# Seven block products in place of eight for 20 chunks of a decoder trunk's last down projection

## The chip, the cores and the metric

The kernel runs on one core of a Trainium2 chip. The metric is the device time of one execution in microseconds (us), and lower is better. A core has a matrix engine (TensorE, PE in the profile, with its weight loads shown as PEld), a vector engine (VectorE, DVE), a scalar engine (ScalarE, ACT), a general-purpose engine (GpSimd, POOL) and a queue engine (SyncE, SP) that issues most of the DMAs here. Each engine works through its own instructions in the order in which the program wrote them, and waits on the others through semaphores.

## The reference, cut to what matters

A two-layer decoder trunk on 256 tokens with width 2048: layer 0 is a gated MLP mixer and a convolutional FFN, then shared keys and values, layer 1 is an attention and a second convolutional FFN, then a final RMSNorm. All of it is float32. The change lies in the last matrix product of all, `w_down` of layer 1:

```python
def conv_ffn(xn, w_up, conv_w, conv_b, w_down):
    h = xn @ w_up                                   # (256, 2048) @ (2048, 11264)
    hp = jnp.pad(h, ((0, 0), (CONV_W - 1, 0), (0, 0)))
    h = sum(hp[:, k:k + S] * conv_w[k] for k in range(CONV_W)) + conv_b
    gate, val = jnp.split(h, 2, axis=-1)
    return (jax.nn.silu(gate) * val) @ w_down       # (256, 5632) @ (5632, 2048)
...
    h = h + conv_ffn(rmsnorm(h, f_norm[l]), f_w_up[l], f_conv_w[l], f_conv_b[l], f_w_down[l])
...
    return rmsnorm(h, final_norm)
```

## The kernel before, in words

**Precision.** Every float32 operand is split into two parts of a shorter format (float32r): a rounded part "hi" and a remainder "lo". A product is the sum of three matmuls: hi x hi, hi x lo and lo x hi. The activations of the second FFN lie in the tile `H` as 44 K-tiles of 128 rows, each with 256 tokens of hi and 256 of lo (`ffn_h`, L642).

**The stream of weights.** All weights come through one `Stream` (L44 to L115) of chunks, 128 x 1024 floats or 512 KB each. SP loads a chunk six items ahead (L77) into one of four `raw` buffers. Three items ahead the chunk is split (L80 to L97): ACT copies it to `whi` (L95), then DVE writes the remainder to `wlo` (L96). Each of `whi` and `wlo` has four buffers, so the split for item i+3 can begin only when PE has finished with the buffer of item i-1. Then PE multiplies item i (L110), and after it `advance` (L63) lets each pending generator emit one more step, up to its next `yield`: the work behind a product (evictions, norms, residuals) is written out in this order among the splits, on the same DVE and ACT queues.

**The down projection of layer 1** (L982 to L985) has 2048 output columns. Three blocks of 512 columns go through `tok_block` (L228 to L272), 22 chunks each, 66 in all. A chunk holds 256 rows of K (two K-tiles) times 512 columns, and its products with the tokens are eight blocks: two K-tiles, two halves of the tokens and two halves of the columns. Each is a 128 x 128 stationary operand of H times a moving 128 x 256 piece of the chunk, in three matmuls: 24 a chunk (a few at the start are 512 wide instead, `wide_next`, L188). The sums stand in a PSUM tile `ps` of two banks, one of three such buffers (`main_ps`, L170). The last 512 columns go in two halves through `short_block` and `last_block` (22 chunks).

**Behind a block** runs `final(blk)` (L407): for each half of the tokens DVE adds `ps` into the residual `h` (L404), ACT takes its square with a running sum (L405), and DVE multiplies by the gain (L416). `output` (L469) closes the kernel.

**GpSimd** is nearly idle: it fills a few constants, masks (L892, `affine_select`) and issues some DMAs of the attention.

**X1**, a tile of 16 x 512 float32r a partition, holds the normed input of the up projection; after the last up product nothing reads it.

Of the kernel before, what the change touches and what calls it, by code (L numbers as in the profile page):

```python
# [22 lines left out]
KF = FFN // P  # L23
NH = 16
CHUNK = 1024
# [6 lines left out]
PAD = 64  # L32
FEAT_AT, TOK_AT = 0, 32
PITCH = 320


C_ANORM, C_KVNORM, C_BNORM, C_FNORM, C_AVNORM = 0, 16, 32, 48, 80
# [6 lines left out]
class Stream:  # L44
# [4 lines left out]
        self.items, self.pending = [], []  # L49
        self.raw, self.parts = {}, {}  # L50

    def chunk(self, src, mult, at, at_load=None, at_split=None, rows=(1, 1), place=None):


        self.items.append((src, mult, at_load, at_split, at, rows, place))

    def then(self, at_load=None, at_split=None, at_mult=None):
        self.items.append((None, at_mult, at_load, at_split, 0, None, None))

    def start(self, gen):  # L60
        self.pending.append(gen)
# [4 lines left out]
                self.pending.remove(g)  # L66

    def _load(self, i):
        src, _, at_load, _, _, _, place = self.items[i]
# [7 lines left out]
        self.nc.sync.dma_start(raw, src)  # L77
        self.raw[i] = raw

    def _split(self, i):  # L80
        if self.items[i][3]:
            self.items[i][3]()
        raw = self.raw.pop(i, None)
        if raw is None:
            return
        at, (n, pitch) = self.items[i][4:6]
        hi, lo = (self.pool.tile([P, CHUNK + PAD], F32R, name=k, tag=k)[:, at:at + CHUNK] for k in ("whi", "wlo"))
# [7 lines left out]
        self.nc.scalar.activation(h, raw, AF.Copy)  # L95
        self.nc.vector.tensor_tensor(l, raw, h.bitcast(F32), op=OP.subtract)  # L96
        self.parts[i] = (hi, lo)  # L97
# [20 lines left out]
class Phase:  # L118
# [22 lines left out]

    def temp(self, key, shape, dtype=F32, bufs=2):
        return self.pool.tile(shape, dtype, name=f"{self.name}_{key}", tag=f"{self.name}_{key}", bufs=bufs)


def build(ctx, tc, d, out):
    nc = tc.nc
# [3 lines left out]
    small = ctx.enter_context(tc.tile_pool(name="small", bufs=1))  # L151
# [6 lines left out]
    X1 = const.tile([P, KD, 2 * T], F32R, name="X1")  # L158
# [17 lines left out]
    def column(i):  # L176
        return col[:, i:i + 1]


    def mm(o, a, b, start, stop):  # L180
        nc.tensor.matmul(o, a, b, start=start, stop=stop, skip_group_check=True)  # L181
# [6 lines left out]
    def wide_next():  # L188
        return state["wide"].pop(0) if state["wide"] else 0
# [38 lines left out]
    def tok_block(src, x, done, K=KD):  # L228
        tok_blocks([(src, done)], x, K)
# [150 lines left out]
    def by_token():  # L380

        return h.rearrange("p a b -> p (a b)").rearrange("p (t f) -> p t f", t=2)
# [17 lines left out]
    def add_block(tb, cols, ps, into):  # L400

        hh = by_token()[:, tb, cols]
        sq = small.tile([P, 2, T], F32, name="sq", tag="sq", bufs=2).rearrange("p a b -> p (a b)")
        nc.vector.tensor_tensor(hh, hh, ps, op=OP.add)  # L404
        nc.scalar.activation(sq[:, :ps.shape[1]], hh, AF.Square, accum_out=into)  # L405

    def final(blk):  # L407
        def done(ps):
            ss = ph.keep("ss", [P, 2, 5])
            n = ps.shape[2]  # L410
            cols = slice(blk * 512, blk * 512 + n)
            for tb in range(2):
                add_block(tb, cols, ps[:, tb, :], ss[:, tb, blk:blk + 1])
                yield
                hh = by_token()[:, tb, cols]
                nc.vector.tensor_tensor(hh, hh, ph.keep("gains", [P, D])[:, cols], op=OP.mult)  # L416
                yield
            if blk == 3:
                v, nv = ph.keep("v", [P, 2]), ph.keep("nv", [P, 2])
                nc.vector.tensor_reduce(v, ss[:, :, :4], axis=AX.X, op=OP.add)  # L420
                nc.vector.tensor_scalar(v, v, 1.0 / D, EPS, op0=OP.mult, op1=OP.add)
                nc.vector.tensor_scalar(nv, v, -0.5, None, op0=OP.mult)
                nc.scalar.activation(warm, ones, AF.Sqrt)
        return done

    def short_block(src, x, K, done):

        n, box = K // 4, {}
        for c in range(n):
            def mult(hi, lo, c=c):  # L430
                if c == 0:
                    box["ps"] = main_ps()[:, :, :T]
                for tb in range(2):
                    short_products(box["ps"][:, tb, :], c, tb, x, K, hi, lo)
                if c == n - 1:
                    s.start(done(box["ps"]))
            s.chunk(src[c], mult, TOK_AT)
        return box
# [203 lines left out]
    def ffn_h():  # L642
        ph.open(f"ffn{state['layer']}")
        return ph.keep("H", [P, KF, 2 * T], F32R)

    def up_done(l, i):
        def done(ps, both):
            state["layer"] = l
            H = ffn_h()
            while state["scaled"] <= l:  # L650
                yield
            a = ph.temp("a", [P, 2, T])
            scaled(ps, both, a)
# [71 lines left out]
    def with_forget(src, x, done):  # L725

        box, n = {}, 0
        for nj in (3, 3, 3, 3, 2, 2):
            def mult(hi, lo, k0=n, nj=nj):
                if k0 == 0:  # L730
                    box["ps"] = main_ps()
                for j in range(nj):
                    kt = k0 + j
                    for tb in range(2):
                        for lower, part in ((0, hi), (0, lo), (1, hi)):
                            at = lower * T + tb * P
# [198 lines left out]
        return done  # L935


    state = {"normed": False, "layer": 0, "v": 0, "done": 0, "gates": 0, "mixed": 0, "scaled": 0, "wide": [8, 2]}
    cd = dram.tile([NH, T], F32, name="cd")

    nc.scalar.dma_start(col[:, :C_KVNORM], d["col"][:, :C_KVNORM])
# [27 lines left out]
    box = short_block(d["kvf_ks"], lambda: att("X2"), KD, lambda ps: iter(()))  # L969
# [85 lines left out]
```

## Time and profile before

| | |
|---|---|
| time, median of 3 runs | 2181.26 us (2180.32 to 2182.49) |
| span of the profiled execution | 2179.9 us, 1.36 us under that median |
| granted TensorE clock | 0.999 |
| matmuls | 18740 |
| HBM read | 430.72 MB, 204 GB/s over the span |

The span is from the first to the last instruction of the one profiled execution; no other time is given for that execution. In the profile's groups, L96 stands for a line of the kernel, `wlo<-raw,whi` for the tiles written and read, and the shapes are partitions x elements; "mean ns" is of one instruction. Matmuls overlap one another, so their cost is read from how many of them a stretch of time holds, and not from the duration of one.

### The profile page before, as it was taken

How to read it: one execution, taken by the hardware profiler on the slowest of the kernel's cores; microseconds unless marked ns; L12 is line 12 of the kernel's file. 1: busy time of each engine (PE TensorE's matmuls, PEld its weight loads, DVE VectorE, ACT ScalarE, POOL GpSimd, SP SyncE). 2: the span in 40 equal slices, each digit the busy share in tenths (PEclk: the TensorE clock that was granted, in tenths of full speed). 3: DMA queues.
4: the chain of work that ended last, by engine and by line, in shares of the span. 5: the costliest groups of instructions: out<-in, count | busy, mean ns of one | idle time of the engine just before them, and what ended most of it. 6: DMA issues, size and time to landing. Idle time of an engine off the chain costs nothing.

```text
span 2179.9 us, 45085 instructions
## 1 busy us (share of the span) xinstructions
PE 2170.3 (100%) x18740; PEld 2154.6 (99%) x18740; DVE 1474.8 (68%) x2085; ACT 1145.4 (53%) x1536; POOL 26.9 (1%) x46
## 2 busy tenths in 40 slices
PE   9999999999999999999999999999999999999998
PEld 9999999999999999999999999999999999999998
DVE  6696687777777755556787676678777777764444
ACT  6665555555555544444545665446555555544443
POOL 0000000000000000000001100000000000000000
PEclk9999999999999999999999999999999999999999
DMA  8686566665666666666777776567766666666664
GB/s 311 191 241 202 193 198 195 189 199 190 198 193 194 195 190 199 193 195 184 244 244 257 232 224 200 185 216 228 240 195 194 193 195 189 201 191 194 193 192 153
DMA packets 153229, 447.31 MB, mean 205 GB/s; under 512 B 25584, under 2 KB 44800, under 8 KB 152640
## 3 DMA queue, kind: packets, MB, share of 16 engines
q1 hardware_dynamic: 151488, 440.48, 64.6%
q0 software_dynamic: 1072, 3.41, 0.6%
q8 instruction: 146, 2.39, 0.5%
q10 hardware_dynamic: 464, 0.55, 0.1%
q14 instruction: 59, 0.48, 0.1%
HBM read 430.72 MB, written 13.65 MB: 204 GB/s over the span
## 4 chain that ended last, share of the span: by engine, by line
PE 99%; DMA 0%; DVE 0%; ACT 0%; SPq 0%; issue 0%; DVEq 0%
PE ps L181 98%; PE mp L913 0%; PE ps L907 0%; PE ps L908 0%; PE ps L906 0%; PE mp L912 0%; DMA mlp_vt<-a_in_v 0%; DVE h L491 0%; PE mp L376 0%; ACT whi L95 0%; ACT sq L405 0%; PE mp L181 0%; DVE h L404 0%; SPq L496 0%; DVE h L486 0%
## 5 line engine op out<-in xcount | busy, mean ns | idle before, releaser
L96 DVE TENSOR_TENSOR wlo<-raw,whi 128x1024 fp32r<-128x1024 f32 (+1 forms) x778 | 945.1, 1219 | 462.4 <-ACT whi L95 458.2
L95 ACT ACTIVATE whi<-raw 128x1024 fp32r<-128x1024 f32 (+1 forms) x778 | 819.3, 1058 | 737.8 <-PE ps L181 660.3
L181 PE MATMUL ps<-X,whi 128*128 128x256 f32 (+1 forms) x6476 | 824.0, 279 | 0.0
L181 PEld LDWEIGHTS ps<-X,whi 128*128 128x128 f32 x6476 | 776.2, 188 | 6.5
L181 PE MATMUL ps<-X,wlo 128*128 128x256 f32 x3328 | 445.3, 276 | 0.0
L181 PEld LDWEIGHTS ps<-X,wlo 128*128 128x128 f32 x3328 | 409.9, 188 | 1.6
L181 PE MATMUL ps<-whi,ffn_H 128*128 128x256 f32 (+1 forms) x1402 | 222.7, 277 | 0.0
L181 PEld LDWEIGHTS ps<-whi,ffn_H 128*128 128x128 f32 x1402 | 192.0, 188 | 0.4
L181 PE MATMUL ps<-ffn_H,whi 128*128 128x256 f32 x1408 | 173.9, 276 | 0.0
L663 DVE SCALAR_TENSOR_TENSOR ffn_c<-ffn_a,col,ffn_c 128x255 f32<-128x255 f32 x352 | 161.9, 481 | 6.4
L181 PEld LDWEIGHTS ps<-ffn_H,whi 128*128 128x128 f32 x1408 | 166.1, 188 | 0.0
L181 PE MATMUL ps<-whi,att_X 128*128 128x256 f32 (+2 forms) x970 | 164.3, 285 | 0.0
L181 PE MATMUL ps<-whi,X 128*128 128x256 f32 (+1 forms) x1000 | 157.4, 280 | 0.4 <-ACT whi L95 0.4
L181 PE MATMUL ps<-wlo,ffn_H 128*128 128x256 f32 (+1 forms) x700 | 151.3, 277 | 0.0
L181 PEld LDWEIGHTS ps<-whi,att_X 128*128 128x128 f32 x970 | 135.4, 188 | 3.5
L181 PEld LDWEIGHTS ps<-whi,X 128*128 128x128 f32 x1000 | 133.5, 188 | 1.9 <-ACT whi L95 0.6
L357 DVE TENSOR_TENSOR ffn_a<-ps,rB 128x512 f32<-128x512 f32 x76 | 52.6, 692 | 116.1 <-PE ps L181 116.1
L659 ACT ACTIVATE ffn_c<-ffn_a,col 128x256 f32<-128x256 f32 x176 | 96.3, 594 | 50.0 <-DVE ffn_a L357 50.0
L181 PEld LDWEIGHTS ps<-wlo,ffn_H 128*128 128x128 f32 x700 | 112.0, 188 | 0.1
L181 PE MATMUL ps<-wlo,att_X 128*128 128x256 f32 (+2 forms) x476 | 105.4, 286 | 0.0
L181 PE MATMUL ps<-wlo,X 128*128 128x256 f32 (+1 forms) x498 | 98.1, 280 | 0.0
L181 PE MATMUL ps<-ffn_H,wlo 128*128 128x256 f32 x704 | 94.1, 276 | 0.0
(177 smaller groups left out, 1379.2 us busy)
## 6 DMA issues: line engine op xcount, KB each, us to landing
raw<-up SPq DMA_DIRECT2D x352, 512.0 KB, 4.1
raw<-down SPq DMA_DIRECT2D x154, 512.0 KB, 4.3
raw<-a_in_u SPq DMA_DIRECT2D x32, 512.0 KB, 4.6
raw<-a_out SPq DMA_DIRECT2D x32, 512.0 KB, 3.9
raw<-b_q SPq DMA_DIRECT2D x32, 512.0 KB, 4.7
raw<-kvf_v SPq DMA_DIRECT2D x32, 512.0 KB, 4.9
raw<-b_g SPq DMA_DIRECT2D x32, 512.0 KB, 4.4
raw<-b_out SPq DMA_DIRECT2D x32, 512.0 KB, 4.2
```

The costliest lines, as they stand in the source:

```text
L95: self.nc.scalar.activation(h, raw, AF.Copy)
L96: self.nc.vector.tensor_tensor(l, raw, h.bitcast(F32), op=OP.subtract)
L181: nc.tensor.matmul(o, a, b, start=start, stop=stop, skip_group_check=True)
L357: nc.vector.tensor_tensor(a, src, rB[:, None, :].to_broadcast([P, 2, T]), op=OP.mult)
L659: nc.scalar.activation(c[:, m, :], a[:, m, :], AF.Identity, scale=w[2], bias=column(C_CONVB + l * 2 * KF + f))
L663: nc.vector.scalar_tensor_tensor(c[:, m, n:], a[:, m, :T - n], w[k], c[:, m, n:], op0=OP.mult, op1=OP.add)
```

## The change

In blocks 0, 1 and 2 of the down projection, 4 + 8 + 8 = 20 of the 66 chunks form their eight block products by a scheme of the Strassen and Winograd kind with seven. Writing A for the tokens' 2 x 2 blocks and B for the chunk's, four sums of A blocks and four of B blocks are made, and seven products of 128 x 128 by 128 x 256.

- *Sums of activations* (`sums_of_blocks`): eight pairs of K-tiles (`SUMMED`), whose four sums in hi and lo fill X1. DVE makes the sums, ACT the hi part, DVE the lo part. They are emitted in 24 steps, one behind each of the first 24 items of block 0.
- *Sums of weights* (`weight_sums`): for each of the 20 chunks GpSimd makes three subtractions from `raw` (512, 256 and 256 elements a partition) into a tile `room`.
- Such a chunk becomes two items: A splits 768 of the raw elements and makes three products (9 matmuls), B splits the 1024 elements of sums and makes four (12 matmuls). B loads nothing.
- Four of the seven products go to a second PSUM tile `m` a block; `sums_into_residual` combines its quarters with ACT and DVE and adds them to the residual in seven steps; `final(blk)` waits in program order until these steps are emitted.
- The order of the chunks is set by `order_of`. With P for a plain chunk and S for one with seven products it gives PPPPPPPPSPPSPPPSPPSPPP in block 0 and PPSPSPPSPSPPSPSPPSPSPP in blocks 1 and 2.
- In `up_done` the temporaries `a` and `c` become halves of one tile `room` of the same size.

```diff
+SUMMED = (4, 5, 8, 9, 12, 13, 16, 17)
+SUMS_ON = lambda nc: nc.gpsimd
...
+    def room(self, at):
+        return [self.pool.tile([P, CHUNK + PAD], F32R, name=k, tag=k)[:, at:at + CHUNK] for k in ("whi", "wlo")]
+
+    def two_parts(self, src, at):
+        n = src.shape[1]
+        hi, lo = self.room(at)
+        self.nc.scalar.activation(hi[:, :n], src, AF.Copy)
+        self.nc.vector.tensor_tensor(lo[:, :n], src, hi[:, :n].bitcast(F32), op=OP.subtract)
+        return hi, lo
...
+def order_of(blk):
+    some = SUMMED[:4] if blk == 0 else SUMMED
+    plain, seven = [c for c in range(KF // 2) if c not in some], list(some)
+    head = 8 if blk == 0 else 2
+    out = [(c, False) for c in plain[:head]]
+    plain = plain[head:]
+    n, m = len(plain), len(seven)
+    for i, c in enumerate(plain):
+        while len(seven) * n > (n - i - 1) * m and seven:
+            out.append((seven.pop(0), True))
+        out.append((c, False))
+    return out
...
     def final(blk):
         def done(ps):
+            while state["summed"] < min(blk + 1, 3):
+                yield
...
+    def sums_of_blocks(q, pair):
+        H = ffn_h()
+        x, f = (small.tile([P, 2, T], F32, name="sq", tag="sq", bufs=2) for _ in range(2))
+        pieces = f.rearrange("p a (b t) -> p (a b) t", b=2)
+        hi, lo = (block_sums()[:, q, :, i, :] for i in range(2))
+        hh = H[:, 2 * pair:2 * pair + 2, :].bitcast(F32)
+        nc.vector.tensor_tensor(x, hh[:, :, :T], hh[:, :, T:], op=OP.add)
...
+        nc.vector.tensor_tensor(s1, a21, a22, op=OP.add)
+        nc.vector.tensor_tensor(s3, a21, a11, op=OP.subtract)
+        yield
+        nc.vector.tensor_tensor(s2, s1, a11, op=OP.subtract)
+        nc.vector.tensor_tensor(s4, a12, s2, op=OP.subtract)
+        nc.scalar.activation(hi, pieces, AF.Copy)
+        yield
+        nc.vector.tensor_tensor(lo, pieces, hi.bitcast(F32), op=OP.subtract)
+        yield
...
+    def weight_sums(raw):
+        t = room()
+        eng = SUMS_ON(nc)
+        eng.tensor_tensor(t[:, :512].rearrange("p (a b) -> p a b", a=2), raw[:, None, :T].to_broadcast([P, 2, T]),
+                          raw[:, T:3 * T].rearrange("p (a b) -> p a b", a=2), op=OP.subtract)
+        eng.tensor_tensor(t[:, 512:768], raw[:, 512:768], t[:, :T], op=OP.subtract)
+        eng.tensor_tensor(t[:, 768:], raw[:, 768:], t[:, 512:768], op=OP.subtract)
+        return t
+
+    def seven_block(blk, src, order, done, sums_done):
...
+        def seven(c, i, first):
...
+            def split(raw):
+                held["t"] = weight_sums(raw)
+                return s.two_parts(raw[:, T:], TOK_AT)
...
+            s.chunk(src[c], mult_plain, TOK_AT, split=split)
+            s.chunk(None, mult_sums, TOK_AT, split=lambda _: s.two_parts(held["t"], TOK_AT))
...
+    def sums_into_residual(blk):
+        def done(m):
...
+            nc.scalar.activation(p1, m[:, 0, :T], AF.Copy)
+            yield
+            nc.vector.tensor_tensor(u, p1, m[:, 0, T:], op=OP.add)
+            nc.vector.tensor_tensor(x, u[:, None, :].to_broadcast([P, 2, T]),
+                                    m[:, 1, :].rearrange("p (a b) -> p a b", a=2), op=OP.add)
+            yield
+            nc.vector.tensor_tensor(u, x[:, 1, :], m[:, 1, :T], op=OP.add)
+            for tb, cols, y in ((0, right, p1), (0, left, x[:, 0, :]), (1, right, x[:, 1, :]), (1, left, u)):
+                nc.vector.tensor_tensor(hh[:, tb, cols], hh[:, tb, cols], y, op=OP.add)
+                yield
+            state["summed"] += 1
         return done
...
+    def room():
+        return ph.temp("room", [P, CHUNK])
...
-            a = ph.temp("a", [P, 2, T])
+            ac = room().rearrange("p (a m t) -> p a m t", a=2, m=2)
+            a, c = ac[:, 0], ac[:, 1]
             scaled(ps, both, a)
             yield
-            c = ph.temp("c", [P, 2, T])
...
     s.then(at_mult=between)
+    s.then(at_mult=lambda: s.start(all_sums()))
     for blk in range(3):
-        tok_block(d["down1"][22 * blk:22 * blk + 22], ffn_h, final(blk), KF)
+        seven_block(blk, d["down1"][22 * blk:22 * blk + 22], order_of(blk), final(blk), sums_into_residual(blk))
```

More of the change, by code (lines that the diff above doesn't have):

```diff
@@ L50, in __init__, with chunk @@
         self.raw, self.parts = {}, {}
-    def chunk(self, src, mult, at, at_load=None, at_split=None, rows=(1, 1), place=None):
-        self.items.append((src, mult, at_load, at_split, at, rows, place))
+    def chunk(self, src, mult, at, at_load=None, at_split=None, rows=(1, 1), place=None, split=None):
+        self.items.append((src, mult, at_load, at_split, at, rows, place, split))
     def then(self, at_load=None, at_split=None, at_mult=None):
-        self.items.append((None, at_mult, at_load, at_split, 0, None, None))
+        self.items.append((None, at_mult, at_load, at_split, 0, None, None, None))
     def start(self, gen):
@@ L68, in _load @@
     def _load(self, i):
-        src, _, at_load, _, _, _, place = self.items[i]
+        src, _, at_load, _, _, _, place, _ = self.items[i]
         if at_load:
@@ L82, in _split @@
             self.items[i][3]()
-        raw = self.raw.pop(i, None)
+        raw, split = self.raw.pop(i, None), self.items[i][7]
+        if split:
+            self.parts[i] = split(raw)
+            return
         if raw is None:
@@ L86, in _split @@
         at, (n, pitch) = self.items[i][4:6]
-        hi, lo = (self.pool.tile([P, CHUNK + PAD], F32R, name=k, tag=k)[:, at:at + CHUNK] for k in ("whi", "wlo"))
+        hi, lo = self.room(at)
         raw = raw.rearrange("p (n w) -> p n w", n=n)
@@ L423, in done, with block_sums @@
                 nc.scalar.activation(warm, ones, AF.Sqrt)
+        return done
+    def block_sums():
+        return X1.rearrange("p (q r) w -> p q (r w)", r=2).rearrange("p q (f l t) -> p q f l t", f=4, l=2)
+    def sums_of_blocks(q, pair):
[5 more added lines that the diff above has]
+        nc.vector.tensor_tensor(x, hh[:, :, :T], hh[:, :, T:], op=OP.add)
+        a11, a21, a12, a22 = (x[:, j, tb * P:(tb + 1) * P] for j in range(2) for tb in range(2))
+        s1, s2, s3, s4 = (pieces[:, i, :] for i in range(4))
+        nc.vector.tensor_tensor(s1, a21, a22, op=OP.add)
[7 more added lines that the diff above has]
+        yield
@@ new lines, in all_sums @@
+    def all_sums():
+        for q, pair in enumerate(SUMMED):
+            yield from sums_of_blocks(q, pair)
+    def weight_sums(raw):
[6 more added lines that the diff above has]
+        return t
@@ new lines, in seven_block, with three, at, plain @@
+    def seven_block(blk, src, order, done, sums_done):
+        x = ffn_h
+        box, last = {}, len(order) - 1
+        lasts = max(i for i, (_, s7) in enumerate(order) if s7)
+        def three(o, parts, stat, j, start, stop):
+            hi, lo = parts
+            for i, (lower, part) in enumerate(((0, hi), (0, lo), (1, hi))):
+                mm(o, stat[lower], part[:, j * T:(j + 1) * T], start and i == 0, stop and i == 2)
+        def at(kt, tb):
+            return [x()[:, kt, lower * T + tb * P:lower * T + (tb + 1) * P] for lower in range(2)]
+        def plain(c, i):
+            def mult(hi, lo):
+                if i == 0:
+                    box["ps"] = main_ps()
+                ps, left = box["ps"], wide_next()
+                for j in range(2):
+                    for tb in range(2):
+                        for lower, part in ((0, hi), (0, lo), (1, hi)):
+                            n, left = 512 if left > 0 else 256, left - 1
+                            for w in range(0, 512, n):
+                                mm(ps[:, tb, w:w + n], x()[:, 2 * c + j, lower * T + tb * P:lower * T + (tb + 1) * P],
+                                   part[:, j * 512 + w:j * 512 + w + n],
+                                   i == 0 and j == 0 and w == 0 and part is hi and not lower,
+                                   i == last and j == 1 and lower == 1)
+                if i == last:
+                    s.start(done(ps))
+            s.chunk(src[c], mult, TOK_AT)
+        def seven(c, i, first):
+            q = SUMMED.index(c)
+            sums = block_sums()[:, q]
+            held = {}
+            def split(raw):
+                held["t"] = weight_sums(raw)
+                return s.two_parts(raw[:, T:], TOK_AT)
+            def mult_plain(hi, lo):
+                if first:
+                    box["m"] = main_ps()
+                m, ps = box["m"], box["ps"]
+                three(m[:, 0, :T], (hi, lo), at(2 * c, 0), 0, first, i == lasts)
+                three(ps[:, 0, T:], (hi, lo), at(2 * c + 1, 0), 2, False, False)
+                three(ps[:, 0, :T], (hi, lo), [sums[:, 3, l, :] for l in range(2)], 1, False, False)
+            def mult_sums(hi, lo):
+                m, ps = box["m"], box["ps"]
+                three(m[:, 1, :T], (hi, lo), [sums[:, 0, l, :] for l in range(2)], 0, first, i == lasts)
+                three(m[:, 1, T:], (hi, lo), [sums[:, 2, l, :] for l in range(2)], 1, False, i == lasts)
+                three(m[:, 0, T:], (hi, lo), [sums[:, 1, l, :] for l in range(2)], 2, False, i == lasts)
+                three(ps[:, 1, T:], (hi, lo), at(2 * c + 1, 1), 3, False, False)
+                if i == lasts:
+                    s.start(sums_done(m))
+            s.chunk(src[c], mult_plain, TOK_AT, split=split)
+            s.chunk(None, mult_sums, TOK_AT, split=lambda _: s.two_parts(held["t"], TOK_AT))
+        for i, (c, s7) in enumerate(order):
+            if s7:
+                seven(c, i, not any(f for _, f in order[:i]))
+            else:
+                plain(c, i)
@@ new lines, in sums_into_residual @@
+    def sums_into_residual(blk):
+        def done(m):
+            hh = by_token()
+            left, right = (slice(blk * 512 + i * T, blk * 512 + (i + 1) * T) for i in range(2))
+            one = room()
+            p1, u, x = one[:, :T], one[:, T:2 * T], one[:, 2 * T:].rearrange("p (a b) -> p a b", a=2)
+            nc.scalar.activation(p1, m[:, 0, :T], AF.Copy)
[9 more added lines that the diff above has]
+            state["summed"] += 1
@@ L935, in g_done @@
         return done
-    state = {"normed": False, "layer": 0, "v": 0, "done": 0, "gates": 0, "mixed": 0, "scaled": 0, "wide": [8, 2]}
+    state = {"normed": False, "layer": 0, "v": 0, "done": 0, "gates": 0, "mixed": 0, "scaled": 0, "summed": 0, "wide": [8, 2]}
     cd = dram.tile([NH, T], F32, name="cd")
```

## The prediction, made before the change was run

> **What bounds the kernel now.** The page comes first: who is busy, and of what the chain that ended last is made.
>
> ```profile
> span 2179.9 us, 45085 instructions
> PE 2170.3 (100%) x18740; PEld 2154.6 (99%) x18740; DVE 1474.8 (68%) x2085; ACT 1145.4 (53%) x1536; POOL 26.9 (1%) x46
> PE 99%; DMA 0%; DVE 0%; ACT 0%; SPq 0%; issue 0%; DVEq 0%
> ```
>
> TensorE sets the time; GpSimd does next to nothing. The chain in order of time says whether that holds in the stretch that changes:
>
> ```profile
> 1461.79 710.41 PE ps L181 x6204
> 2172.22 0.43 DVE h L404
> ```
>
> From 1461.79 to 2172.2 us nothing but matmuls is on it: the last up projection and the whole down projection run without a gap. So a matmul less there is worth its cadence, as long as nobody makes TensorE wait. The busy times by stretch give the cadence:
>
> ```profile
> 1996.00:2054.00 58.00, 58.00 (x514) 58.00 (x513) 28.41 (x26) 23.13 (x26) 0.00 (x0) 1.00 0.64 194
> ```
>
> That row's columns are PE, PEld, DVE, ACT, POOL, clock, DMA share and GB/s. It holds 514 matmuls in 58 us, 0.1128 us each at full clock. A plain chunk of 24 is 2.71 us, a chunk of 21 is 2.37 us: 1.015 for item A's nine, 1.354 for item B's twelve. VectorE is busy for just under half of it. What one chunk asks of the other engines, from the groups of the last 230 us (the last is a square into a running sum, with its read-out):
>
> ```profile
> L96 DVE TENSOR_TENSOR wlo<-raw,whi 128x1024 fp32r<-128x1024 f32 x79 | 96.8, 1225 | 107.6 <-ACT whi L95 107.6
> L95 ACT ACTIVATE whi<-raw 128x1024 fp32r<-128x1024 f32 x79 | 83.8, 1061 | 107.5 <-PE ps L181 102.5 <-ACT whi L95 3.5 <-issue 1.3
> L404 DVE TENSOR_TENSOR h<-h,ps 128x512 f32<-128x512 f32 x6 | 4.1, 684 | 1.2 <-PE ps L181 1.2
> L404 DVE TENSOR_TENSOR h<-h,ps 128x256 f32<-128x256 f32 x4 | 1.7, 419 | 5.5 <-PE ps L181 5.5
> L405 ACT ACTIVATE sq<-h 128x512 f32<-128x512 f32 x6 | 3.8, 632 | 13.7 <-DVE h L404 13.7
> L405 ACT ACTIVATION_READ_ACCUMULATOR sq<-h 128x1 f32 x10 | 1.9, 186 | 0.0
> ```
>
> Both engines wait for each other in a ring: ACT for PE's release of `whi`, VectorE for ACT. How far ahead of TensorE that ring runs is the cover on which everything rests:
>
> ```profile
> 2003.63 1.06 ACT L95 ACTIVATE whi<-raw 128x1024 fp32r<-128x1024 f32 x1 [1.65 <-PE ps L181]
> 2004.73 1.23 DVE L96 TENSOR_TENSOR wlo<-raw,whi 128x1024 fp32r<-128x1024 f32 x1 [1.33 <-ACT whi L95]
> ```
>
> The copy begins as PE ends item i-1, and the remainder is ready at 2005.96, 2.33 us later. This is item i+3's, which PE reaches after three chunks, 8.1 us: the cover is 5.8 us. Among seven-product chunks three items in a row (A, B, P) last only 1.015 + 1.354 + 2.71 = 5.08 us, and the cover can be no more than about 2.8 us.
>
> **The change part by part.**
>
> *Removed.* 20 chunks lose 3 matmuls each: 60 x 0.1128 = 6.8 us, all on the path. That is the whole gain to be had, 0.31% of 2181.26.
>
> *Splits.* A plain chunk costs VectorE one L96. A seven-product chunk costs two: 768 elements in A, by the line through 0.684 (512) and 1.225 (1024) about 0.955 us, and 1024 in B. How they stand in a queue:
>
> ```profile
> 1178.82 0.71 DVE L692 STREAM_TRANSPOSE att_turned<-att_big 128x512 f32<-128x512 f32 x1
> 1179.45 1.19 DVE L96 TENSOR_TENSOR wlo<-raw,whi 128x1024 fp32r<-128x1024 f32 x1
> ```
>
> The second starts 0.08 before the first ends, so back to back A is 0.875, B and P 1.145 us.
>
> *Sums of weights, on GpSimd.* No subtraction by GpSimd is in this trace. The nearest rows are masks, with one input:
>
> ```profile
> L948 POOL TENSOR_SCALAR_AFFINE_SELECT ident<-ident 128x128 f32<-128x128 f32 x1 | 0.3, 287 | 0.1
> 1231.27 0.52 DVE L864 SCALAR_TENSOR_TENSOR att_big<-mp,att_big 128x384 f32<-128x384 f32 x1
> 1231.29 0.40 POOL L892 TENSOR_SCALAR_AFFINE_SELECT att_big<-att_big 128x256 f32<-128x256 f32 x1 [10.70 <-issue]
> ```
>
> 128 elements take 0.287 and 256 take 0.40 us: 0.174 fixed and 0.88 ns an element. Three instructions with 1024 elements are 0.52 + 0.90 = 1.43 us if a second input costs nothing, and 2.33 us if it doubles the pace. I take 2.33, since the engine has to fetch twice as much. The Trainium skill, "GPSIMD Engine Reference", section on performance versus the Vector engine, has 4497 ns for a two-input instruction of 2048 elements; an estimate from it is 2.25 us a chunk, which no run here shows, and the sum by it would be at most 1.6 us (20 x 0.08) lower.
>
> In that fence GpSimd's mask runs beside a VectorE instruction that reads PSUM, undisturbed. Beside a split it doesn't:
>
> ```profile
> 1192.40 0.40 POOL L892 TENSOR_SCALAR_AFFINE_SELECT att_big<-att_big 128x256 f32<-128x256 f32 x1 [10.07 <-ACT att_big L890]
> 1192.46 1.43 DVE L96 TENSOR_TENSOR wlo<-raw,whi 128x1024 fp32r<-128x1024 f32 x1
> ...
> 1217.67 1.48 POOL L892 TENSOR_SCALAR_AFFINE_SELECT att_big<-att_big 128x256 f32<-128x256 f32 x1 [10.75 <-issue]
> 1217.67 1.21 DVE L96 TENSOR_TENSOR wlo<-raw,whi 128x1024 fp32r<-128x1024 f32 x1
> ```
>
> Where the mask came first, the split took 1.43 in place of 1.225; where both came at once, the mask took 1.48 in place of 0.40 and ended 0.27 after the split. Split and GpSimd's read take turns, whole instructions at a time. So GpSimd's 2.33 us a chunk are no free work beside VectorE: they are added to the queue of everything in which VectorE reads two tiles of SBUF, and that is all splits and all new sums. The Trainium skill says so too, "SBUF — State Buffer", section "Who interferes with whom": of a VectorE instruction with two SBUF inputs and a GpSimd instruction that reads SBUF, the second to issue blocks until the first is done. The trace agrees (1.48 beside 0.40); taken strictly it puts the sum at the upper ends below, against this change.
>
> *Block 0.* The sums of activations are emitted behind its 24 first items, 8 of them before the first S. For a pair of K-tiles: two instructions of 512 (0.684) and four of 128, by the line through 0.419 and 0.684 about 0.286 each, 2.51 less three overlaps of 0.08, 2.27 us of VectorE. In between stands a turn: the ACT copy of 512 waits for VectorE's last sum (0.63, as L405's square), the next `whi` copy stands behind it on ACT (1.06), the next split waits for that: 1.69 us in which VectorE stands idle once it has no cover. Behind the eight head chunks this fits (1.145 + 0.76 an item in 2.71). The next 16 items, 4 A, 4 B, 8 P, last 4 x 2.37 + 8 x 2.71 = 31.1 us on PE. VectorE has 4 x 0.875 + 12 x 1.145 = 17.2 of splits and 16/3 x 2.27 = 12.1 of sums, 29.3; GpSimd takes turns for 4 x 2.33 = 9.3; the turns with ACT come to 16/3 x 1.69 = 9.0. If GpSimd's work falls exactly into those turns, 29.3 + 9.3 = 38.6, and after the cover of 5.8 TensorE waits 1.7 us. If none of it does, 47.6 and a wait of 10.7. I take the middle, 6.2: a turn has room for the first of the three instructions or the other two, but they come when a load has landed, not when a turn begins.
>
> *Heads of blocks 1 and 2.* There the new residual work (`sums_into_residual`: one addition of 512, six of 256) fills the few plain chunks that should rebuild the cover, and `final` of the block before is moved past it to the first seven-product rounds. In A B P A B P, 10.2 us of PE, VectorE has splits of 2 x (0.875 + 2 x 1.145) = 6.3 and `final`'s four of 0.684, 2.4 less overlaps; GpSimd 4.7: 13.4. Each of `final`'s two squares holds ACT for 0.632 + 0.186, with the next copy behind it: two turns of 1.88, 3.8. With the cover of 2.8 whole and the turns filled the wait is 0.4 us; with the turns empty 4.2; with no cover left after block 0 as well 7.0. I take 3.7 for block 1 (the middle of 0.4 and 7.0) and 2.3 for block 2 (of 0.4 and 4.2). The rounds after that hold: S P S P P is 12.9 us of PE against 7.5 + 4.7 = 12.2.
>
> *At nothing.* `m`, a second PSUM tile a block: with three buffers, the next block's `m` finds the buffer of the last one, read out before that block ends. Loads: the same bytes in the same order on SP, whose four buffers now wait for GpSimd as well.
>
> ```profile
> SPq L77 <- DVE wlo L96: 168.2, 73, 3.6
> raw<-down SPq DMA_DIRECT2D x55, 512.0 KB, 4.3
> ```
>
> SP waits for the splits, and a load lands in 4.3 us; with four buffers a load goes out three chunks ahead, over 7 us, and 3 are left. If splits run late the loads do too, which is in the upper ends. `room` in `up_done` replaces two tiles of the same total: nothing. Blocks after block 2 change only by `final(2)`, with eleven plain chunks to hide it: nothing, and if not, its four instructions, 2.7 us.
>
> **Sum.** -6.8 + 6.2 + 3.7 + 2.3 = +5.4 us: span 2185.3, and with the 1.36 us by which the median stands over the profiled span, **2186.7 us**. With all the lower ends (1.7 + 0.4 + 0.4) it is -4.3, 2177.0; with GpSimd at 1.43 as well, no wait is left and it is -6.8, 2174.5. With all the upper ends (10.7 + 7.0 + 4.2) it is +15.1, 2196.4.
>
> **The rivals.**
>
> *The cover holds, faster.* The place is VectorE's turns with ACT in block 0: if GpSimd's three instructions fit them, or cost nearer 1.43 than 2.33, waits stay under 2.4 us and over 4.4 us of the gain arrive. It gives 2174.5 to 2177.0, say 2176. For it: VectorE's 29.3 alone is under 31.1. Against: nothing steers GpSimd into the turns. Decisive is whether GpSimd's time and VectorE's in those 16 items add to less than 31.1 + 5.8 + 2.4 = 39.3 us. Chance 0.22.
>
> *Block 0 waits, the heads don't.* 6.2 + 0.4 + 0.4 against 6.8: +0.2, 2181.5, no change. For it: GpSimd may finish early, ahead of the rounds with `final`. Chance 0.28.
>
> *GpSimd itself is late.* If each of its instructions meets a split and waits 1.08 (1.48 less 0.40), a chunk's sums take 2.33 + 3.24 = 5.6 us, more than an S P round's 5.08, and B's copy on ACT waits for them with the next chunks' copies behind it. That is the top, 2196 or more. Against: S P S P P gives it 12.9 us for 11.1. Chance 0.12, a part of the 0.50 for slower.
>
> **How the numbers follow.** 0.2%, 4.4 us, is about what a measurement of this kernel can tell from no change. The forecast and the late GpSimd make slower 0.50, of which the forecast has 0.38; the second rival 0.28 same; the first 0.22 faster. The range from 2175.5 to 2196.0 leaves out a bare tenth at the top and a little at the bottom; the likeliest case's own range is 2185.7 to 2196.
>
> **What would show it.** Matmuls: 18680, 60 fewer. PE idle in front of L181 in the down projection, with ACT L95 or DVE L96 as releaser: some 12 us, half of it in the last two thirds of block 0, the rest at the heads of blocks 1 and 2, none later. GpSimd's subtractions: alone about 1.07 and 0.62 us, beside splits longer by up to 1.1, and splits among them at 1.4 and over. VectorE busy over 90% in block 0 behind its eighth chunk. The prediction is wrong if PE's idle time stays under 3 us, if GpSimd and splits overlap at their lone durations, or if the wait stands at a PSUM tile or a load.

## The result and the profile after

The changed kernel takes 2199.02 us (2198.44 to 2201.8) against 2181.23, a ratio of 1.0084 (95% interval 1.0070 to 1.0097): 17.8 us slower, where 5.4 slower was forecast and 2196.0 was the top of the range. Two single executions further down that ran at a granted clock of 0.58 and 0.80 (3707 and 2575 us) are left out of every median and ratio. The page of the profile after, first its span, engines and chain:

```profile
span 2196.7 us, 45186 instructions
PE 2172.4 (99%) x18680; PEld 2152.2 (98%) x18680; DVE 1546.5 (70%) x2174; ACT 1163.2 (53%) x1567; POOL 110.3 (5%) x106
PE 95%; DVE 3%; issue 1%; ACT 1%; DMA 1%; POOL 0%; ACTq 0%; DVEq 0%; POOLq 0%
```

The 60 matmuls are gone (18680 after 18740), so the change does what it says. But TensorE, 99% of the chain before, is 95% of it now. Most of the rest is VectorE (3%) and ACT; the 1% of DMA is a load of `b_q` in the attention, far from the change, and GpSimd itself has 0%. The busy times by stretch (columns PE, PEld, DVE, ACT, POOL, clock, DMA share, GB/s) tell where:

```profile
1951.00:2000.00 49.00, 40.55 (x317) 38.50 (x317) 39.13 (x55) 20.00 (x24) 13.09 (x9) 0.97 0.46 142
2000.00:2031.00 31.00, 26.44 (x215) 24.86 (x213) 25.53 (x26) 14.28 (x19) 15.91 (x12) 1.00 0.50 154
2031.00:2062.00 31.00, 30.86 (x270) 30.78 (x271) 24.93 (x19) 16.11 (x17) 18.62 (x13) 1.00 0.64 212
2062.00:2092.00 30.00, 28.23 (x243) 27.64 (x242) 23.63 (x24) 15.69 (x20) 14.03 (x12) 1.00 0.58 181
2092.00:2122.00 30.00, 30.00 (x267) 30.00 (x266) 24.37 (x18) 15.13 (x16) 17.85 (x12) 1.00 0.65 201
```

A busy PE is not a PE at its pace, so the matmuls are counted, at 0.1128 us each as before. In 1951 to 2000, the mixed part of block 0, 317 matmuls are worth 35.8 us: 13.2 are lost. In 2000 to 2031, the head of block 1, 215 are 24.3: 6.7 lost. The same reckoning gives 0.5 in the next stretch, 2.6 in the head of block 2 and nothing behind it. Together 23.0, less the 6.8 saved, is 16.2; the span grew by 16.8. Not all of it is idle time: the waits of TensorE's matmuls come to 14.7 us, all of them for VectorE (13.3) or ACT (1.4). The last section accounts for some 1.5 us of the rest by a lower clock; how the others divide is not shown.

The groups of the last 267 us of the kernel after show what the instructions had become (L112 is the split of a plain chunk, L96 before; L90 the splits of A and B; L492 to L495 GpSimd's subtractions; L471 and L481 the sums of activations):

```profile
L112 DVE TENSOR_TENSOR wlo<-raw,whi 128x1024 fp32r<-128x1024 f32 x67 | 92.8, 1390 | 41.2 <-ACT whi L111 41.1
L492 POOL TENSOR_TENSOR ffn_room<-raw 128x512 f32<-128x512 f32 x20 | 30.1, 1505 | 576.9 <-DMA raw<-down 551.5 <-DVE wlo L90 14.1 <-DVE wlo L112 11.1
L494 POOL TENSOR_TENSOR ffn_room<-raw,ffn_room 128x256 f32<-128x256 f32 x20 | 28.2, 1410 | 1.6
L90 DVE TENSOR_TENSOR wlo<-raw,whi 128x768 fp32r<-128x768 f32 x20 | 26.6, 1331 | 4.6 <-ACT whi L89 4.6
L90 DVE TENSOR_TENSOR wlo<-ffn_room,whi 128x1024 fp32r<-128x1024 f32 x20 | 26.6, 1329 | 11.7 <-ACT whi L89 11.7
L495 POOL TENSOR_TENSOR ffn_room<-raw,ffn_room 128x256 f32<-128x256 f32 x20 | 25.4, 1272 | 1.6
L471 DVE TENSOR_TENSOR sq<-ffn_H 128x512 f32<-128x512 f32 x8 | 7.7, 957 | 0.0
L481 DVE TENSOR_TENSOR X<-sq,X 128x512 fp32r<-128x512 f32 x8 | 7.1, 891 | 0.0
```

A split of 1024 has a mean of 1.39 us after 1.225, one of 768 takes 1.33 where 0.955 was reckoned, and the 512-element sums 0.89 to 0.96 where 0.684 was. GpSimd's three come to 1.505 + 1.410 + 1.272 = 4.19 us a chunk. How such a duration comes about stands in the timeline (start, length):

```profile
1969.55 1.23 DVE L112 TENSOR_TENSOR wlo<-raw,whi 128x1024 fp32r<-128x1024 f32 x1 [1.65 <-ACT whi L111]
1969.72 2.23 POOL L492 TENSOR_TENSOR ffn_room<-raw 128x512 f32<-128x512 f32 x1 [10.55 <-DMA raw<-down]
...
1970.69 1.80 DVE L481 TENSOR_TENSOR X<-sq,X 128x512 fp32r<-128x512 f32 x1
...
1972.03 1.07 POOL L494 TENSOR_TENSOR ffn_room<-raw,ffn_room 128x256 f32<-128x256 f32 x1
1972.42 1.76 DVE L112 TENSOR_TENSOR wlo<-raw,whi 128x1024 fp32r<-128x1024 f32 x1
...
1974.10 1.22 DVE L471 TENSOR_TENSOR sq<-ffn_H 128x512 f32<-128x512 f32 x1
...
2079.98 0.75 POOL L494 TENSOR_TENSOR ffn_room<-raw,ffn_room 128x256 f32<-128x256 f32 x1
2080.81 0.75 POOL L495 TENSOR_TENSOR ffn_room<-raw,ffn_room 128x256 f32<-128x256 f32 x1
```

The split ends at 1970.78; only then does GpSimd's subtraction get on, until 1971.95; only then VectorE's L481, until 1972.49. Each is charged with the other's time. The last two rows met nobody: 0.75 us for 256 elements. The three lengthened VectorE rows are 1.1, 0.5 and 0.5 us over what they take alone (0.685, 1.225 and 0.686), 2.2 us for this chunk; the same working over all four seven-product chunks of block 0 gives 8.3 us.

### The profile page after: what moved, and what is told of

Its sections match the earlier page's. It is cut to its first block, busy times and chain, and to the rows that moved or that the text cites. A ratio compares the mean times of both kernels' runs of the same rounds, so it can differ in the third digit from the quotient of the medians.

```text
span 2196.7 us, 45186 instructions
## 1 busy us (share of the span) xinstructions
PE 2172.4 (99%) x18680; PEld 2152.2 (98%) x18680; DVE 1546.5 (70%) x2174; ACT 1163.2 (53%) x1567; POOL 110.3 (5%) x106
## 3 DMA queue, kind: packets, MB, share of 16 engines
q0 software_dynamic: 1072, 3.41, 0.6%
## 4 chain that ended last, share of the span: by engine, by line
PE 95%; DVE 3%; issue 1%; ACT 1%; DMA 1%; POOL 0%; ACTq 0%; DVEq 0%; POOLq 0%
PE ps L213 94%; DVE wlo L112 1%; DVE wlo L90 1%; DMA raw<-b_q 1%; ACT whi L111 0%; PE mp L1076 0%; DVE X L481 0%; DVE sq L471 0%; PE mp L684 0%; PE ps L1070 0%; PE ps L1071 0%; PE ps L1069 0%; PE mp L1075 0%; ACT whi L89 0%; DVE h L450 0%
## 5 line engine op out<-in xcount | busy, mean ns | idle before, releaser
L112 DVE TENSOR_TENSOR wlo<-raw,whi 128x1024 fp32r<-128x1024 f32 x758 | 932.8, 1236 | 391.9 <-ACT whi L111 387.7
L111 ACT ACTIVATE whi<-raw 128x1024 fp32r<-128x1024 f32 x758 | 796.8, 1057 | 656.4 <-PE ps L213 566.4
L213 PE MATMUL ps<-whi,ffn_H 128*128 128x256 f32 (+1 forms) x1202 | 199.2, 278 | 0.6 <-ACT whi L111 0.6
L213 PE MATMUL ps<-whi,X 128*128 128x256 f32 (+1 forms) x1160 | 188.7, 280 | 0.8 <-ACT whi L89 0.8
L826 DVE SCALAR_TENSOR_TENSOR ffn_room<-ffn_room,col 128x255 f32<-128x255 f32 x352 | 161.9, 481 | 6.4
L213 PEld LDWEIGHTS ps<-whi,X 128*128 128x128 f32 x1160 | 159.2, 188 | 2.6 <-ACT whi L89 1.0
L389 DVE TENSOR_TENSOR ffn_room<-ps,rB 128x512 f32<-128x512 f32 x76 | 52.6, 692 | 116.1 <-PE ps L213 116.1
L213 PE MATMUL ps<-wlo,X 128*128 128x256 f32 (+1 forms) x578 | 121.0, 281 | 3.5 <-DVE wlo L90 3.2
L822 ACT ACTIVATE ffn_room<-ffn_room,col 128x256 f32<-128x256 f32 x176 | 96.3, 595 | 50.0 <-DVE ffn_room L389 50.0
L213 PEld LDWEIGHTS ps<-wlo,ffn_H 128*128 128x128 f32 x600 | 99.9, 189 | 13.2 <-DVE wlo L112 12.6
L213 PEld LDWEIGHTS ps<-wlo,X 128*128 128x128 f32 x578 | 90.0, 188 | 5.1 <-DVE wlo L90 4.3
```

## The experiments

Ten kernels. Each ratio is to the kernel before, measured on the same chip. Theory 1: GpSimd's reads and VectorE's two-input instructions exclude each other. Beside it stands the suspicion of the turns, in which VectorE waits for ACT and ACT for VectorE. Theory 2: VectorE has too much work, GpSimd is a bystander. Theory 3: GpSimd's sums are late whatever VectorE does.

**The sums on VectorE.**

```diff
-SUMS_ON = lambda nc: nc.gpsimd
+SUMS_ON = lambda nc: nc.vector
```

> VectorE makes the weights' sums in place of GpSimd; all else as in the changed kernel. VectorE then has some 1.3 us more a seven-product chunk (one subtraction of 512, two of 256, at 0.684 and 0.419 less overlaps). Theory 1, the two engines exclude each other whenever VectorE reads two tiles of SBUF and GpSimd reads too: the splits come back to 1.225 and 0.955 us, the time to about 2185 us (2180 to 2189), because the turns between VectorE and ACT in block 0 remain. Theory 2, VectorE simply has too much new work and GpSimd is only a bystander: 26 us more on VectorE make it slower still, 2199 to 2210.

2188.66 us (five executions, 2188.46 to 2194.75), ratio 1.0037 (1.0024 to 1.0051). With 20 x (0.685 + 0.425 + 0.426) = 31 us more work on VectorE the kernel is 10 us faster than with GpSimd, and the groups, from the slowest of the five, have the splits back:

```profile
L112 DVE TENSOR_TENSOR wlo<-raw,whi 128x1024 fp32r<-128x1024 f32 x34 | 41.3, 1221 | 16.8 <-ACT whi L111 16.4
L90 DVE TENSOR_TENSOR wlo<-raw,whi 128x768 fp32r<-128x768 f32 x18 | 17.1, 952 | 0.0
L492 DVE TENSOR_TENSOR ffn_room<-raw 128x512 f32<-128x512 f32 x17 | 11.6, 685 | 0.0
```

Theory 2 falls in its plain form. The time lies at the top of what theory 1 gave (2189), so a good part of the loss is not exclusion.

**GpSimd writes and doesn't read.**

```diff
-        eng.tensor_tensor(t[:, :512].rearrange("p (a b) -> p a b", a=2), raw[:, None, :T].to_broadcast([P, 2, T]),
-                          raw[:, T:3 * T].rearrange("p (a b) -> p a b", a=2), op=OP.subtract)
-        eng.tensor_tensor(t[:, 512:768], raw[:, 512:768], t[:, :T], op=OP.subtract)
-        eng.tensor_tensor(t[:, 768:], raw[:, 768:], t[:, 512:768], op=OP.subtract)
+        for _ in range(3):
+            eng.memset(t, 0.0)
```

> GpSimd fills the sums' tile three times with zeros in place of the three subtractions, so the seven-product chunks' sums of weights are left out. It writes as often and, by the fill of 128 elements in 0.205 us, needs some 2.85 us alone, against 2.82 for the three subtractions where nothing met them, but it reads nothing from SBUF. Theory 1, exclusion by reads: no split is held up, about 2179 us (2176 to 2183). Theory 3, GpSimd's sums are late for item B whatever VectorE does: the fills are as late, 2195 to 2200.

2180.54 us, ratio 0.9997 (0.9987 to 1.0006): 18 us faster than the changed kernel, with GpSimd busy for 3 x 0.957 = 2.87 us a chunk.

```profile
L112 DVE TENSOR_TENSOR wlo<-raw,whi 128x1024 fp32r<-128x1024 f32 x50 | 60.9, 1223 | 33.4 <-ACT whi L111 32.9
L493 POOL MEMSET ffn_room<- 128x1024 f32 x57 | 54.5, 957 | 107.8 <-DVE wlo L90 88.3 <-DVE ffn_H L316 15.1 <-DVE h L579 2.3
L90 DVE TENSOR_TENSOR wlo<-raw,whi 128x768 fp32r<-128x768 f32 x20 | 19.1, 955 | 10.7 <-ACT whi L89 10.7
```

Splits and fills lie side by side and neither is longer for it: it is the reading that excludes. One thing more changes here: a fill need not wait for the load, so it starts earlier than a subtraction could. The run clears exclusion and lateness away together; that exclusion stretches the instructions is seen in the rows above.

**No sums of activations.**

```diff
-    s.then(at_mult=lambda: s.start(all_sums()))
+    s.then(at_mult=lambda: None)
```

> The sums of activations are left out (the products read what X1 held before), GpSimd's sums of weights stay. Theory 1 with the turns between VectorE and ACT: block 0's 13 us of waits nearly go, the heads of blocks 1 and 2 keep some 9 us or a little less, about 2184 us (2181 to 2188). Theory 3, GpSimd late whatever VectorE does: only the products' inputs change, all 20 chunks still wait, over 2194 us.

2182.16 us, ratio 1.0005 (0.9996 to 1.0014). All 20 chunks still have GpSimd's subtractions, and 17 us are gone; theory 3 falls. GpSimd's reads without the sums of activations (this run) eat 7.7 us, about the saving of 6.8; those sums without GpSimd's reads (the fills above) eat 6.1. What costs 24.6 is both at the same time.

**Exclusion alone, under the old cover.** Every chunk has its 24 matmuls; GpSimd makes the sums, and nobody reads them.

```diff
-                seven(c, i, not any(f for _, f in order[:i]))
+                plain(c, i, (lambda raw: (weight_sums(raw), s.two_parts(raw, TOK_AT))[1]) if s7 else None)
...
-    s.then(at_mult=lambda: s.start(all_sums()))
...
-            while state["summed"] < min(blk + 1, 3):
-                yield
```

> The kernel before, with 24 matmuls in every chunk, and GpSimd making the same three subtractions for the same 20 chunks, whose result nobody reads. Theory 1: splits that meet GpSimd take up to 1.75 us and GpSimd up to 2.2, as in the changed kernel, but the cover of 5.8 us takes it all: 2181 us, within 1 us of before. If exclusion alone were enough to stop TensorE it would be 2190 or more. If GpSimd and splits do not meet here at all, the splits stay at 1.225.

2181.81 us, ratio 1.0001 (0.9992 to 1.0011), as forecast. The meetings are there:

```profile
L112 DVE TENSOR_TENSOR wlo<-raw,whi 128x1024 fp32r<-128x1024 f32 x48 | 67.3, 1403 | 62.4 <-ACT whi L111 62.4
L490 POOL TENSOR_TENSOR ffn_room<-raw 128x512 f32<-128x512 f32 x20 | 37.4, 1871 | 553.6 <-DMA raw<-down 553.6
```

With one split a chunk and a cover of 5.8 us they cost nothing. In these runs exclusion hurts only where the cover is used up.

**The turn taken out, GpSimd kept.** The same instructions. The last two VectorE sums of a pair move from the second of its three steps into the first, so ACT's copy, still in the second, stands one step behind the sums that it needs.

```diff
         nc.vector.tensor_tensor(s3, a21, a11, op=OP.subtract)
-        yield
         nc.vector.tensor_tensor(s2, s1, a11, op=OP.subtract)
         nc.vector.tensor_tensor(s4, a12, s2, op=OP.subtract)
+        yield
         nc.scalar.activation(hi, pieces, AF.Copy)
```

> GpSimd as in the changed kernel. Of each pair's sums of activations, the last two VectorE sums are made in the first step, and ACT's copy stands a step later, behind the next chunk's copy, so that ACT no longer waits for VectorE's newest sum with the next copy behind it. No instruction is added or left out. If the turns between ACT and VectorE (1.69 us a pair, eight pairs) are the second half of block 0's waits, the time falls by 6 to 10 us from the changed kernel, to about 2190 us (2187 to 2193), and what is left is exclusion. If only the amount of work counts, it stays within 2 us of 2199.

2188.54 us, ratio 1.0034 (1.0022 to 1.0047): 10.5 us faster than the changed kernel. The stretches of block 0 and of block 1's head:

```profile
1951.00:2000.00 49.00, 47.02 (x400) 46.03 (x399) 45.43 (x64) 24.00 (x29) 17.27 (x12) 1.00 0.59 183
2000.00:2031.00 31.00, 26.88 (x225) 25.79 (x224) 24.95 (x21) 13.74 (x18) 18.51 (x13) 1.00 0.56 171
```

400 matmuls in place of 317: block 0 loses 3.9 us where it lost 13.2; block 1's head still loses 5.6.

**Both.** That order, and the sums on VectorE:

> The same order, and VectorE makes the weights' sums. If exclusion and turns are two causes that add, both are gone: about 2183 us (2180 to 2186), against 2189 to 2190 with VectorE alone. VectorE's queue in block 0 is still over full: 29.3 us of splits and sums of activations plus 4 x 1.4 of sums of weights against 31.1 of TensorE. If the turns were only a by-product of exclusion, it stays at 2189.

2181.71 us, ratio 1.0007 (0.9998 to 1.0017), as forecast: no gain and no loss in the median. Three of the ten executions took 2184.8 to 2187.3; why is not shown.

**Both, and the chunks spread.** For the two kernels that follow:

```diff
-    some = SUMMED[:4] if blk == 0 else SUMMED
+    some = SUMMED[:2] if blk == 0 else SUMMED
...
-    head = 8 if blk == 0 else 2
+    head = 14 if blk == 0 else 8
```

> As the last, and the seven-product chunks are moved away from the two places that wait: block 0 has two of them behind 14 plain chunks, blocks 1 and 2 keep eight but behind 8 plain chunks. 18 chunks save 54 matmuls, 6.1 us. If only the two places (the sums of activations, and the heads of blocks with final and the residual sums) lack cover, nearly all of it arrives: about 2176 us (2175 to 2179). If seven-product chunks on VectorE cost cover anywhere, 2180 or more.

> The same order and places with GpSimd making the weights' sums. The only difference to the run before is the engine of 54 subtractions. Exclusion costs cover everywhere: 2182 us (2179 to 2185), some 6 us slower than with VectorE. If the places alone mattered, it would be the same 2176.

On VectorE 2178.38 us, ratio 0.9988 (0.9978 to 0.9997), on GpSimd 2180.73, ratio 0.9999 (0.9990 to 1.0009). Both lie in their ranges, but VectorE's is 2 us slower than its number, and the step between them is 2.4 us, not 6; with intervals that overlap, even this step's size is uncertain. Eight seven-product chunks behind eight plain ones stand in pairs (PPPPPPPPSSPSPSPSSPSPSP), and behind such pairs the chain of the VectorE kernel runs over VectorE's three sums, ACT's copy of them and the next split, again and again. VectorE is busy for only 80 to 83% of the two stretches that lose matmuls (2031 to 2062 and 2092 to 2122), so this looks like a turn between two engines more than a full queue; no run separates the two. In the GpSimd kernel POOL has 1% of the chain: there the six subtractions of a pair, one behind the other, are on the path, so in pairs GpSimd's lateness counts too.

**Both causes away, all 20 chunks in their places**: the fills, and ACT's copy a step behind the sums.

> Both suspected causes away, all 20 seven-product chunks in their places: GpSimd writes zeros three times and reads nothing (the sums of weights are left out), and ACT's copy of the activations' sums stands a step later. If exclusion and the turns in block 0 are all that ate the gain, nearly the whole 6.8 us arrives: 2175 us (2174.4 to 2177). If a third cause is left (the second split a chunk, the residual's sums, the loads), it stays at 2178 or more.

2175.66 us, ratio 0.9977 (0.9968 to 0.9986): 6.0 of the 6.8 us arrive. In the median no third cause of any size is left; but three of the eleven executions took 2178.2 to 2181.3, and no trace shows why. With the changed kernel (+17.8), the fills alone (-0.7 against the before of their call), the turn alone (+7.3) and this (-6.0) the two causes can be weighed: GpSimd's reading (exclusion, and whatever of its lateness a fill doesn't have) costs 18.5 us with the turns in place and 13.3 without; the turns 10.5 with it and 5.3 without. Some 5 us of the loss belong to neither alone.

**Sixteen chunks, VectorE.** Fewer, and spread so that none stand in pairs:

```diff
-SUMMED = (4, 5, 8, 9, 12, 13, 16, 17)
+SUMMED = (4, 5, 8, 9, 12, 13, 16)
-SUMS_ON = lambda nc: nc.gpsimd
+SUMS_ON = lambda nc: nc.vector
...
-    some = SUMMED[:4] if blk == 0 else SUMMED
+    some = SUMMED[:2] if blk == 0 else SUMMED
...
-    head = 8 if blk == 0 else 2
+    head = 14 if blk == 0 else 7
```

> VectorE makes the weights' sums, ACT's copy a step later, and 16 seven-product chunks: two in block 0 behind 14 plain chunks, seven each in blocks 1 and 2 behind seven. 48 matmuls are 5.4 us. With more plain chunks between, the cover should hold everywhere: 2176 us (2175 to 2178), faster than with 18 in spite of two savings less. If VectorE's sums cost cover at any density, it is 2178 or more.

2175.89 us (2175.46 to 2176.42), ratio 0.9974 (0.9963 to 0.9985): the fastest kernel that does the whole work, 5.7 us under the kernel before, for 48 matmuls at 5.4. Its stretches hold every matmul that fits:

```profile
1951.00:2000.00 49.00, 49.00 (x434) 49.00 (x434) 40.32 (x65) 23.78 (x26) 0.00 (x0) 1.00 0.64 204
2000.00:2031.00 31.00, 31.00 (x276) 31.00 (x275) 25.80 (x35) 16.59 (x20) 0.00 (x0) 1.00 0.59 177
...
2062.00:2092.00 30.00, 30.00 (x267) 30.00 (x266) 25.95 (x35) 15.48 (x18) 0.00 (x0) 1.00 0.56 175
```

VectorE is 82 to 87% busy in these rows, and TensorE never waits for it.

## Why the prediction was right in kind and wrong in size

*The gain.* 6.8 us for 60 matmuls: right. 6.0 of it came with both causes away, in a kernel that leaves out the sums of weights.

*Who would be in the way.* Right: exclusion between splits and GpSimd's reads, and the turns between VectorE and ACT, at the places named: block 0 and the heads of blocks 1 and 2. The upper ends were 10.7, 7.0 and 4.2 us; measured were 13.2, 6.7 and 2.6 to 3.1, in all 23.0 against 21.9. The rule of the Trainium skill in "SBUF — State Buffer", section "Who interferes with whom", taken strictly, was put there at these upper ends. Its other half, that a GpSimd instruction that only writes does not contend, is what the fills show (0.957 us each beside splits of 1.223).

*The step that failed* is the wait of block 0: "If GpSimd's work falls exactly into those turns ... If none of it does, 47.6 and a wait of 10.7. I take the middle, 6.2". None of it did: in block 0 none of the seven turns from 1942 to 1996 meets any of the four chunks' subtractions. The timeline of the kernel after at one turn, and GpSimd's next instruction:

```profile
1951.52 0.29 DVE L478 TENSOR_TENSOR sq<-sq 128x128 f32<-128x128 f32 x1
1951.84 0.63 ACT L479 ACTIVATE X<-sq 128x512 fp32r<-128x512 f32 x1 [6.06 <-DVE sq L478]
...
1953.24 0.96 DVE L90 TENSOR_TENSOR wlo<-raw,whi 128x768 fp32r<-128x768 f32 x1 [1.44 <-ACT whi L89]
...
1954.97 2.13 POOL L492 TENSOR_TENSOR ffn_room<-raw 128x512 f32<-128x512 f32 x1 [5.18 <-DMA raw<-down]
```

VectorE stands idle for 1.44 us, the turn reckoned at 1.69; and GpSimd stands idle too, for 5.18 us, because its load has not landed. In the rows shown above it is the same (1.65 us of turn before 1969.55, while GpSimd waited 10.55 for a load) and then both want to read at once. Three of the four chunks wait for a load, the fourth for a split of the item before it. The loads go out when a split frees a buffer, and nothing ties their landing to a gap; that this is why none fell into one is argued and not shown by a run. Splitting the difference between two ends was no estimate: what had to be asked is what starts GpSimd's work, and the wait list for SP had shown that it is the splits.

With nothing in the turns the prediction's own sum gives 10.7, still short of 13.2. The second thing that failed is the cover. The prediction let the mixed part begin with all 5.8 us of it ("Behind the eight head chunks this fits"). In the trace it is gone at the first seven-product chunk. The split of its item B, and TensorE waiting for just this split, and then for the next one:

```profile
1954.72 1.22 DVE L90 TENSOR_TENSOR wlo<-ffn_room,whi 128x1024 fp32r<-128x1024 f32 x1
...
1955.99 0.19 PEld L213 LDWEIGHTS ps<-wlo,X 128*128 128x128 f32 x1 [0.33 <-DVE wlo L90]
...
1960.30 0.69 PE L213 MATMUL ps<-wlo,ffn_H 128*128 128x256 f32 x2 [2.56 <-DVE wlo L112]
```

From 1935 to 1951, in the head, VectorE was busy for 14.18 of 16 us and stood in a turn for 1.65 of the rest: the last work of the up projection, the sums of activations and the first chunk's meetings with GpSimd (2.1 us) left no room to rebuild it.

*The size of a subtraction.* The bounds of 1.43 and 2.33 us a chunk did not hold it. Alone, the 256-element subtraction takes 0.75 us (above) and the 512-element one 1.32:

```profile
2040.76 1.32 POOL L492 TENSOR_TENSOR ffn_room<-raw 128x512 f32<-128x512 f32 x1
```

1.32 + 0.75 + 0.75 = 2.82. It is tempting to put this into block 0's sum: 29.3 + 9.0 + 4 x 2.82 = 49.6, and after 31.1 and 5.8 a wait of 12.7, against 13.2 measured. That it comes so near is luck: two errors nearly cancel. VectorE was held up by 2.0 to 2.2 us a chunk and not by 2.82, less even than the 2.33 of the prediction, for only three chunks in those 16 items, 6.3 us; and there was hardly any cover. With the trace's figures the sum is 29.3 + six turns of 9.5 in all + 6.3 = 45.1, and after 31.1 a wait of 14.0, against 13.2 in a stretch that is not cut exactly at these items. So the terms were the right ones, but the turns stood empty and the cover was not there.

*The heads.* 3.7 us forecast for block 1 and 6.7 measured, just under the upper end of 7.0, which was the one with no cover left after block 0: the same error; for block 2 2.3 forecast and 2.6 to 3.1 measured.

*The rivals.* "The cover holds" and "block 0 waits, the heads don't" did not come. "GpSimd itself is late" came in part: its three instructions took 4.19 us, not 5.6, and ACT waited 25.0 us for them in all, but with the turns away ACT waits 27.4 and the kernel is 10.5 us faster, so this wait is not the price by itself. Nor is GpSimd's lateness on the chain of the kernel after (POOL 0%). The list of waits of the kernel after:

```profile
ACT whi L89 <- POOL ffn_room L495: 25.0, 13, 3.3
...
PE ps L213 <- DVE wlo L112: 10.1, 10, 2.6
```

*At nothing.* The PSUM tile, `room` in `up_done` and the bytes of the loads stayed at nothing; the loads' timing did not, as told. TensorE waits for no load and no PSUM tile in these stretches.

*A sign that failed.* VectorE was to be busy over 90% in block 0 behind its eighth chunk. It is 80% (39.13 of 49 us), because it stands in the turns: an engine can set the pace without being full.

## What to carry to other kernels

Before work goes to an engine that is "idle anyway", ask what it reads, which instructions of the busy engine it excludes, and what starts it: here it waited for loads and splits, and none of it fell into the busy engine's gaps in block 0. In a ring of two engines, look for the place where one has an instruction that needs the other's newest result ahead of work that is ready; one `yield` moved was worth 10 us here. Before a cover is counted on, check that it is still there where the change begins. And a saving that is paid in cover is best taken in fewer places: with the sums on VectorE and the turn taken out, 16 chunks, spread out, saved 5.7 us where 20 in the first places saved nothing.

## What the runs showed of the hardware that was not expected

GpSimd with two inputs from SBUF: 0.75 us for 256 and 1.32 for 512 elements a partition, which is 2.2 ns an element and 0.18 us fixed, two and a half times what its one-input mask takes for an element (0.88 ns), not twice. The Trainium skill's figure in "GPSIMD Engine Reference", section on performance versus the Vector engine, gives about the same pace (4497 ns for 2048 elements), but the estimate from it left out the 0.18 us of each of three instructions. In the stretch with the longest waits the granted clock was 0.97. In finer stretches that is one piece of 3.41 us at half the clock, right behind one in which TensorE did little:

```profile
1957.04:1960.45 3.41, 0.85 (x8) 0.65 (x7) 3.37 (x5) 0.00 (x0) 1.97 (x3) 1.00 0.05 18
1960.45:1963.86 3.41, 3.41 (x17) 3.41 (x18) 1.74 (x3) 3.06 (x4) 0.00 (x0) 0.50 0.52 154
```

17 matmuls at 0.1128 us would take 1.9 us, so some 1.5 of the 13.2 us is slower matmuls and not idle time. The kernels with the sums on VectorE in the first order, without the sums of activations, and with the turn out and the sums on VectorE each show one such piece too, behind 3.41 us in which TensorE was busy for 1.75, 1.60 and 1.85; behind one, in the second of these kernels, in which it was busy for 2.93, the clock stayed at 1.00.
